# The four products of a conditioning step, side by side in the tensor engine's order

## The chip, the cores and the metric

The kernel runs on one core of a Trainium2 chip. The metric is the device time of one execution in microseconds (us); the median of three executions before the change is 3292.84 us. Five engines work beside one another: TensorE (PE in the profile; PEld is its weight load), VectorE (DVE), ScalarE (ACT), GpSimd (POOL) and SyncE (SP, which here issues all the DMA transfers; SPq is its queue). Each takes its own instructions in the order in which the program queues them.

## The reference, cut to what matters

Two transformer layers run over 1024 latent tokens and 256 context tokens, 1024 wide, in fp32. Every norm is followed by a shift, a scale and a gate that come from two conditioning vectors, one for the latent tokens and one for the context:

```python
s_x = jax.nn.silu(c)
s_c = jax.nn.silu(c_ctx)
for l in range(DEPTH):
    mod_x = (s_x @ w_mod[l] + b_mod[l])[:, None, :]
    mod_c = s_c @ w_mod[l] + b_mod[l]
    sh1_x, sc1_x, g1_x, sh2_x, sc2_x, g2_x = jnp.split(mod_x, 6, axis=-1)
    ...
    x = x + g1_x * rms_norm(m_x, norm_g[l, 1])
    f_x = squared_relu_mlp(modulate(rms_norm(x, norm_g[l, 2]), sh2_x, sc2_x), w_mlp_in[l], w_mlp_out[l])
    x = x + g2_x * rms_norm(f_x, norm_g[l, 3])
```

`w_mod[l]` is 1024 x 6144. The change is about the products `s @ w_mod` alone; the rest of the kernel computes the mixers and the MLPs.

## The kernel before

Almost all large products are dense ones: `dense()` (L377 to L384) multiplies tiles that were split into a high and a low part, three TensorE matmuls per step of 128 (L382, L383, L384), each as a rule 512 columns wide. The profile shows these as `mm`.

The conditioning products come in **rounds** (`mod_round`, L218): six of them, three per layer, each for 2048 of the 6144 columns. A round has 8 **steps**, one per 128 rows of `w_mod`. A step loads two tiles of weights, v = 0 and v = 1 (L239, SyncE's queue), 1024 columns each, and makes four products (L243 to L247): two of 512 columns from each tile. The stationary operand is `s2[:, k, :]`, 32 columns wide, of which two hold the conditioning vectors. Product g = 2v + h writes PSUM partitions 32g to 32g + 32 of one bank, `md`, and so uses columns 32g to 32g + 32 of the TensorE array. The four of a step therefore use four different column strips. A step's loop goes v = 0 first, then v = 1. The operands are plain fp32, and each product leaves two records in the trace. At the end of a round VectorE adds the biases and gains (L253 to L257), TensorE transposes the result (L260) and VectorE copies it to `mcols`, or it goes to DRAM as rows.

The rounds are spread over three stages. Round 0 of layer 0 is made in the prologue, in two halves: `parts` is ((0,), (1,)), so that a step there has two products and two tiles of 512 columns, in 32 buffers of their own. Rounds 1 and 2 of layer 0 are made in the in-projection: `rounds()` (L273) hands out one step for every third tile of tokens. The three rounds of layer 1 are made in layer 0's MLP, one step for every fifth tile, which is two steps in each of the first twelve blocks of 256 hidden columns. In these last two stages the weight tiles sit in `stg`, two staging buffers of 128 x 1024 (NSTG = 2), which the weights of the dense products (`ws`, L353) use too. A dense weight tile is read from staging by ScalarE (L186) and GpSimd or VectorE (L193), which make its high and low parts.

The order of each engine's queue is set when the program is built: a scheduler takes, at each point of its own simulated time, the ready instruction of the highest priority, and priorities follow the order in which the program was written. Nothing ties the four products of a step together, and other ready matmuls can come between them. The two places where the order is written by hand are the attention and the last block of each MLP; the rounds' products are in neither.

Of the kernel before, what the change touches and what calls it, by code (L numbers as in the profile page):

```python
# [129 lines left out]
def hybrid_dit_kernel(ctx: ExitStack, tc: tile.TileContext, x, c, cx, c_ctx, w_mod, b_mod, norm_g, w_in,  # L130
# [3 lines left out]
    pe, act, dve, pool, sp = nc.tensor, nc.scalar, nc.vector, nc.gpsimd, nc.sync  # L134
# [8 lines left out]
    def dscr(shape, name, dt=F32):  # L143
        return dram.tile(shape, dt, name=name)
# [51 lines left out]
    s2 = const.tile([128, 8, 32], F32, name="s2")  # L196
# [21 lines left out]
    def mod_round(l, r, ps, tmp, tmp_bufs, parts=((0, 1),)):  # L218

        pt = ps.tile([128, 512], F32, name="md", tag="md", bufs=1)  # L220
        bg = stg.tile([128, 2, 512], F32, tag="bg", name="bg", bufs=1)
        bt, gt = bg[:, 0, :], bg[:, 1, :]
        def biases():
            for g in range(4):
                sp.dma_start(bt[32 * g:32 * g + 32, :],
                             b_mod[l:l + 1, r * 2048 + g * 512:r * 2048 + (g + 1) * 512].to_broadcast([32, 512]))
                i = KIND[2 * r + g // 2]
                if i is not None:
                    sp.dma_start(gt[32 * g:32 * g + 32, :],
                                 norm_g[l, i:i + 1, (g % 2) * 512:(g % 2 + 1) * 512].to_broadcast([32, 512]))  # L230

        for hs in parts:
            n, h0 = 512 * len(hs), hs[0]
            for k in range(8):
                ws = []
                for v in range(2):
                    w = tmp.tile([128, n], F32, tag="stg", name="wm", bufs=tmp_bufs)
                    c0 = r * 2048 + v * 1024 + h0 * 512
                    sp.dma_start(w, w_mod[l, k * 128:(k + 1) * 128, c0:c0 + n])  # L239
                    ws.append(w)  # L240
                if hs is parts[0] and k == BIAS_AT:
                    biases()
                for v in range(2):  # L243
                    for h in hs:
                        g = 2 * v + h
                        pe.matmul(pt[32 * g:32 * g + 32, :], s2[:, k, :], ws[v][:, (h - h0) * 512:(h - h0 + 1) * 512],  # L246
                                  start=(k == 0), stop=(k == 7))  # L247
                yield
            for v in range(2):
                i = KIND[2 * r + v]  # L250
                p = slice(64 * v + 32 * h0, 64 * v + 32 * (hs[-1] + 1))
                a, g = bt[p, :], gt[p, :]
                dve.tensor_tensor(a, pt[p, :], a, op=OP.add)  # L253
                if i in (0, 2):
                    dve.scalar_tensor_tensor(a, a, 1.0, g, op0=OP.add, op1=OP.mult)
                elif i in (1, 3):
                    dve.tensor_tensor(a, a, g, op=OP.mult)  # L257
            tr = ps.tile([128, 512], F32, name="tr", tag="tr", bufs=3)
            for k in range(4):
                pe.transpose(tr[:, k * 128:(k + 1) * 128], bt[:, k * 128:(k + 1) * 128], ident)  # L260
            tr = tr.rearrange("p (k g s) -> p g s k", k=4, g=4)
            for v in range(2):
                i = 2 * r + v
                if i in (2, 5):
                    rows[l, i] = dscr([2, 2, 512], f"rows{l}{i}")
                    for s in range(2):
                        for g in range(2):
                            sp.dma_start(rows[l, i][s, g:g + 1], bt[64 * v + 32 * g + s:64 * v + 32 * g + s + 1, :])
                else:
                    for h in hs:  # L270
                        dve.tensor_copy(mcols[:, 2 * l + i // 3, i % 3, :, 4 * h:4 * h + 4], tr[:, 2 * v + h, 0:2, :])

    def rounds(l, rs, ps, every):  # L273

        steps = (x for r in rs for x in mod_round(l, r, ps, stg, NSTG))
        n = [0]

        def tick():
            n[0] += 1
            if n[0] % every == 0:  # L280
                next(steps, None)
        return tick
# [1053 lines left out]
    with tc.tile_pool(name="ps0", bufs=1, space=PSUM, reuse_waits="tile") as ps:  # L1336
        outs[0] = ex.enter_context(tc.tile_pool(name="tq", bufs=1, reuse_waits="tile"))
        with tc.tile_pool(name="tn", bufs=1, reuse_waits="tile") as tmp:
# [11 lines left out]
            with tc.tile_pool(name="m0", bufs=1, side="right", reuse_waits="tile") as m0:  # L1350
                cond_vectors(ps)
                steps = mod_round(0, 0, ps, m0, 32, ((0,), (1,)))
                for _ in range(8):
                    next(steps)
                xs = [load_x(t, ("mm", 4)) for t in al[:NF]]
                next(steps)
                for t, xt in zip(al, xs):
                    half(0, t, xt, act)
                W0 = Weights(0, True)
                loads = W0.starts(w_in[0], 1792, 512, dve)  # L1360
                for go in loads[:2]:
                    go()()
                for _ in steps:
                    pass
                for go in loads[2:]:
                    go(dve)()
# [464 lines left out]
```

## Time and profile before

| | us |
|---|---|
| median of three executions | 3292.84 |
| lowest and highest of the three | 3285.52, 3294.04 |
| the profiled execution | 3286.25 |
| its span, first to last instruction | 3284.4 |
| TensorE busy in the span | 3196.6 |
| VectorE, ScalarE, GpSimd busy | 1547.1, 1117.9, 1056.1 |

The profile's page gives busy time by engine; its views then go by stretch (each engine's busy time and TensorE's granted clock, 1.00 being 2.4 GHz), by line, and by time. In the rows by time one row is one instruction, or several of one kind that follow one another, with its start, its length and, in brackets, the idle time before it and what ended that. The lengths of matmuls overlap: what one costs in a row of them is read from start to start.

### The profile page before, as it was taken

The page shows a single profiled execution, that of the slowest core. Times are in us where ns is not written, and L with a number is a line of the kernel's source. Part 1 is how long each engine was busy: PE and PEld are TensorE (multiplying, and loading weights), DVE is VectorE, ACT ScalarE, POOL GpSimd, SP SyncE. Part 2 cuts the span into 40 slices and gives each one's busy share as a digit, 9 for nine tenths or more (in the row PEclk, how much of TensorE's full clock was granted, in tenths as well). Part 3 has the DMA queues.
Part 4 walks back from the last instruction along what each step waited for, and adds up shares of the span by engine and source line. Part 5 has one row for each costly group of instructions (what it writes and reads, how often), then busy time and mean ns, then how long its engine had stood idle before and what let it go on. Part 6 is the DMA issues. An engine that isn't in the chain of part 4 may idle for free.

```text
span 3284.4 us, 47529 instructions
## 1 busy us (share of the span) xinstructions
PE 3196.6 (97%) x18421; PEld 2611.4 (80%) x18421; DVE 1547.1 (47%) x3295; ACT 1117.9 (34%) x2315; POOL 1056.1 (32%) x878
## 2 busy tenths in 40 slices
PE   8999999999999999999999989999989999999997
PEld 3777888887887777777778878998878788888886
DVE  3345476798462343343343561148755333333335
ACT  4212576788342111111111242257864311111111
POOL 2346100035452232232232453210334533333333
PEclk9999999999999999999999999999999999999999
DMA  7566312132432222222121146124454211111113
GB/s 242 166 150 177 81 53 57 55 85 87 138 116 84 71 63 84 64 71 85 57 65 39 58 145 153 44 60 118 130 152 127 73 45 52 52 45 51 46 46 96
DMA packets 221569, 294.00 MB, mean 90 GB/s; under 512 B 36800, under 2 KB 154064, under 8 KB 221344
## 3 DMA queue, kind: packets, MB, share of 16 engines
q1 hardware_dynamic: 221248, 290.71, 30.0%
q8 instruction: 145, 2.38, 0.3%
q14 instruction: 80, 0.66, 0.1%
q0 software_dynamic: 96, 0.26, 0.0%
HBM read 240.01 MB, written 50.89 MB: 89 GB/s over the span
## 4 chain that ended last, share of the span: by engine, by line
PE 75%; DVE 3%; issue 2%; DMA 2%; POOL 1%; ACT 1%; SPq 0%; POOLq 0%; ACTq 0%; DVEq 0%
PE mm L382 20%; PE mm L383 19%; PE mm L384 19%; PE po L1081 2%; PE tp L1060 2%; PE po L913 2%; PE md L246 1%; PE S L515 1%; PE X L516 1%; PE X L515 1%; PE S L516 1%; PE po L808 1%; PE tp L892 1%; PE tp L790 1%; POOL s L193 1%
## 5 line engine op out<-in xcount | busy, mean ns | idle before, releaser
L1198 DVE TENSOR_TENSOR acc<-mm,acc 128x512 f32<-128x512 f32 x540 | 369.1, 689 | 388.1 <-PE mm L384 387.1
L193 POOL TENSOR_TENSOR r<-ws,r 128x1024 fp32r<-128x1024 f32 x146 | 356.9, 2449 | 539.5 <-ACT r L186 534.8
L384 PE MATMUL mm<-s,r 128*128 128x512 f32 (+1 forms) x1404 | 516.6, 368 | 0.0
L383 PE MATMUL mm<-s,r 128*128 128x512 f32 (+1 forms) x1404 | 515.5, 367 | 0.0
L382 PE MATMUL mm<-s,r 128*128 128x512 f32 (+1 forms) x1404 | 513.5, 366 | 1.7 <-DVE s L188 1.7
L1184 DVE TENSOR_TENSOR hr<-hr 128x512 f32<-128x512 f32 (+1 forms) x160 | 134.4, 840 | 612.7 <-ACT hr L1183 612.6
L382 PE MATMUL mm<-r,r 128*128 128x512 f32 x1046 | 413.5, 395 | 0.3 <-DVE r L188 0.3
L383 PE MATMUL mm<-r,r 128*128 128x512 f32 x1046 | 408.5, 391 | 0.0
L384 PE MATMUL mm<-r,r 128*128 128x512 f32 x1046 | 407.9, 390 | 0.0
L186 ACT ACTIVATE r<-ws 128x1024 fp32r<-128x1024 f32 x155 | 164.4, 1061 | 709.2 <-PE mm L384 336.8
L193 POOL TENSOR_TENSOR r<-hr,r 128x512 fp32r<-128x512 f32 (+1 forms) x130 | 167.0, 1285 | 562.6 <-DVE r L188 559.2
L1183 ACT ACTIVATE hr<-mm 128x512 f32<-128x512 f32 (+1 forms) x160 | 88.3, 552 | 644.4 <-PE mm L384 638.4
L382 PEld LDWEIGHTS mm<-s,r 128*128 128x128 f32 x1404 | 264.2, 188 | 50.6 <-DVE s L188 1.9
L383 PEld LDWEIGHTS mm<-s,r 128*128 128x128 f32 x1404 | 264.7, 189 | 49.2
L384 PEld LDWEIGHTS mm<-s,r 128*128 128x128 f32 x1404 | 264.1, 188 | 46.1
L382 PEld LDWEIGHTS mm<-r,r 128*128 128x128 f32 x1046 | 196.2, 188 | 80.7 <-DVE acc L1198 36.9
L384 PEld LDWEIGHTS mm<-r,r 128*128 128x128 f32 x1046 | 196.3, 188 | 43.0 <-POOL r L193 0.9
L383 PEld LDWEIGHTS mm<-r,r 128*128 128x128 f32 x1046 | 196.4, 188 | 39.1
L713 ACT ACTIVATE P<-P,nm 128x1280 f32<-128x1280 f32 (+1 forms) x160 | 190.2, 1190 | 31.1 <-DVE P L721 28.7
L382 PE MATMUL mm<-r,e 128*128 128x512 f32 (+1 forms) x496 | 192.6, 389 | 1.3 <-ACT e L186 1.3
L383 PE MATMUL mm<-r,e 128*128 128x512 f32 (+1 forms) x496 | 190.9, 385 | 0.0
L384 PE MATMUL mm<-r,e 128*128 128x512 f32 (+1 forms) x496 | 189.8, 385 | 0.4 <-POOL e L193 0.4
(256 smaller groups left out, 6011.3 us busy)
## 6 DMA issues: line engine op xcount, KB each, us to landing
wm<-in_w_mod_dram SPq DMA_DIRECT2D x80, 512.0 KB
ws<-in_w_mlp_in_dram SPq DMA_DIRECT2D x64, 512.0 KB
ws<-in_w_mlp_out_dram SPq DMA_DIRECT2D x64, 512.0 KB
q<-qT SPq DMA_DIRECT2D x224, 128.0 KB
ws<-in_w_in_dram SPq DMA_DIRECT2D x36, 512.0 KB
xres<-xn SPq DMA_DIRECT2D x18, 512.0 KB
x<-xres SPq DMA_DIRECT2D x18, 512.0 KB
wm<-in_w_mod_dram SPq DMA_DIRECT2D x32, 256.0 KB
```

The source lines that it names most:

```text
L186: act.activation(o, i, AF.Copy)
L193: lo_eng.tensor_tensor(lo, src, f(hi), op=OP.subtract)
L382: pe.matmul(pt, sh, mh, start=k == 0, stop=False)
L383: pe.matmul(pt, sh, ml, start=False, stop=False)
L384: pe.matmul(pt, sl, mh, start=False, stop=k == n - 1)
L515: pe.matmul(dst, q[0], k, start=True, stop=False)
L516: pe.matmul(dst, q[1], k, start=False, stop=True)
L713: act.activation(P, P, AF.Exp, scale=-1.0, bias=self.nm[:, u:u + 1], accum_out=self.sums[:, u:u + 1])
L913: pe.matmul(self.po, VB[self.h][:, kt, :], self.pt[:, kt, :], start=kt == self.kts[0], stop=kt == self.kts[-1])
L1183: act.activation(r, pt, AF.Relu)
L1184: dve.tensor_tensor(r, r, r, op=OP.mult)
L1198: dve.tensor_tensor(acc[t][:, s], pt, acc[t][:, s], op=OP.add)
```

## The change

In `mod_round` the four products of a step are made in the order v = 1, v = 0. The first of them keeps the place that its priority gives it. The other three are given a high priority, and each gets an edge that queues it on TensorE behind the first one (order of issue only, no wait for its end).

```diff
-                for v in range(2):
-                    for h in hs:
-                        g = 2 * v + h
-                        pe.matmul(pt[32 * g:32 * g + 32, :], s2[:, k, :], ws[v][:, (h - h0) * 512:(h - h0 + 1) * 512],
-                                  start=(k == 0), stop=(k == 7))
+
+                def group(v, h):
+                    g = 2 * v + h
+                    return pe.matmul(pt[32 * g:32 * g + 32, :], s2[:, k, :],
+                                     ws[v][:, (h - h0) * 512:(h - h0 + 1) * 512], start=(k == 0), stop=(k == 7))
+                gs = [(v, h) for v in (1, 0) for h in hs]
+                with tc.high_priority(), tc.issue_after(group(*gs[0]).ins):
+                    for x in gs[1:]:
+                        group(*x)
                 yield
```

`issue_after` adds the edges; `high_priority` raises the priority of what is traced inside it.

## Rows read from the trace of the kernel before

**Rows 1.** The page's first part: busy us, share of the span, instructions.

```profile
PE 3196.6 (97%) x18421; PEld 2611.4 (80%) x18421; DVE 1547.1 (47%) x3295; ACT 1117.9 (34%) x2315; POOL 1056.1 (32%) x878
```

**Rows 2.** Busy time by stretch (us), TensorE's clock, DMA share: prologue, in-projection, MLP.

```profile
25.00:57.00 32.00, 29.81 (x96) 11.94 (x96) 9.71 (x16) 10.15 (x25) 9.09 (x8) 0.95 0.57 206
85.00:330.00 245.00, 239.96 (x1350) 186.93 (x1350) 107.45 (x231) 54.83 (x128) 121.45 (x144) 0.99 0.59 162
985.00:1685.00 700.00, 700.00 (x3229) 536.09 (x3228) 249.55 (x371) 93.18 (x131) 189.78 (x115) 1.00 0.24 74
```

**Rows 3.** In-projection and MLP again, L246's instructions alone (PE and PEld).

```profile
85.00:330.00 245.00, 24.15 (x128) 3.35 (x128) 0.99 0.59 162
985.00:1685.00 700.00, 51.54 (x192) 7.04 (x192) 1.00 0.24 74
```

**Rows 4.** TensorE in order of time, one step in layer 0's MLP.

```profile
1053.05 0.39 PE L384 MATMUL mm<-r,r 128*128 128x512 f32 x1
1053.37 1.05 PE L246 MATMUL md<-wm,s 128*32 128x512 f32 x4
1054.35 0.50 PE L382 MATMUL mm<-r,r 128*128 128x512 f32 x1
1054.69 0.39 PE L383 MATMUL mm<-r,r 128*128 128x512 f32 x1
1054.92 0.39 PE L384 MATMUL mm<-r,r 128*128 128x512 f32 x1
...
1055.94 1.05 PE L246 MATMUL md<-wm,s 128*32 128x512 f32 x4
1056.93 0.50 PE L382 MATMUL mm<-r,r 128*128 128x512 f32 x1
```

**Rows 5.** TensorE in order of time, one step in the in-projection.

```profile
184.11 0.40 PE L384 MATMUL mm<-r,e 128*128 128x512 f32 x1
184.44 1.07 PE L246 MATMUL md<-wm,s 128*32 128x512 f32 x8
185.44 0.50 PE L382 MATMUL mm<-r,e 128*128 128x512 f32 x1
185.77 0.39 PE L383 MATMUL mm<-r,e 128*128 128x512 f32 x1
```

**Rows 6.** TensorE in order of time, end of the prologue's second half round.

```profile
52.77 1.05 PE L246 MATMUL md<-wm,s 128*32 128x512 f32 x2
53.74 0.50 PE L382 MATMUL mm<-r,e 128*128 128x512 f32 x1
...
59.14 0.66 PE L260 MATMUL tr<-ident,bg 128*128 128x128 f32 x4 [1.86 <-DVE bg L255]
```

**Rows 7.** TensorE in order of time, two groups of L246 that a transfer held up.

```profile
18.67 2.34 PE L246 MATMUL md<-wm,s 128*32 128x512 f32 x6 [1.05 <-DMA wm<-in_w_mod_dram]
...
262.25 1.92 PE L246 MATMUL md<-wm,s 128*32 128x512 f32 x4 [2.47 <-DMA wm<-in_w_mod_dram]
```

**Rows 8.** L246's weight loads: ns shortest, median, longest; first and last start.

```profile
L246 PEld LDWEIGHTS md<-wm,s x384: 106/109/178, 4.7 to 1671.1; 128*32 128x32 f32 x192
```

**Rows 9.** Layer 0's MLP: issues on SyncE's queue, in order of time.

```profile
1046.02 11.34 SPq L239 DMA_DIRECT2D wm<-in_w_mod_dram  x4
1063.72 2.90 SPq L353 DMA_DIRECT2D ws<-in_w_mlp_out_dram  x2
```

**Rows 10.** The MLP's weight tiles and their users on ScalarE, GpSimd and TensorE.

```profile
1067.24 1.06 ACT L186 ACTIVATE r<-ws 128x1024 fp32r<-128x1024 f32 x1 [22.06 <-DMA ws<-in_w_mlp_out_dram]
...
1071.15 2.39 POOL L193 TENSOR_TENSOR r<-ws,r 128x1024 fp32r<-128x1024 f32 x1 [0.32 <-ACT r L186]
...
1104.10 4.93 POOL L193 TENSOR_TENSOR r<-ws,r 128x1024 fp32r<-128x1024 f32 x2 [0.45 <-ACT r L186]
...
1104.23 0.39 PE L382 MATMUL mm<-r,r 128*128 128x512 f32 x1
...
1142.43 0.60 ACT L1183 ACTIVATE hr<-mm 128x512 f32<-128x512 f32 x1 [10.90 <-PE mm L384]
```

## The prediction

> **What bounds the kernel now.** I read the page's busy times first: TensorE works for 97% of the span, no other engine for half of it [rows 1]. The share is an average, so next came the stretches in which the rounds lie. In the MLP of layer 0, from 985 to 1685 us, TensorE is busy 700.00 of 700 us at the full clock, and VectorE, ScalarE and GpSimd for 250, 93 and 190; the transfers take 0.24 of the DMA engines' time. In the in-projection TensorE is busy 239.96 of 245 us, in the second part of the prologue 29.81 of 32 [rows 2]. Where one engine has no idle time and feeds the rest, its work is the time: what comes off its queue comes off the span. The third view is that queue itself, in order of time, around L246, and it shows what a group of these products costs. By start to start, dense matmuls follow each other every 0.23 us (1054.69 to 1054.92). With a group between them, L384 starts at 1053.05 and the second dense matmul behind the group at 1054.69: 1.64 us where two pitches would be 0.46. So **a group of two products costs 1.18 us** [rows 4]. A step in the in-projection whose four products happen to stand together spans 184.11 to 185.77, 1.66 us, so **a group of four costs 1.20 us** [rows 5]. A single product holds the queue from 52.77 to 53.74, 0.97 us, as long as two do (0.98) [rows 4, 6]. The price belongs to the group, not to the product: those on different column strips run at the same time, and 0.2 us of each group lies at its two borders with the dense matmuls.
>
> **How many groups the change removes.** Each x in these rows counts records, two per product, so x4 is half a step, x8 a whole one.
>
> MLP: 192 records [rows 3], 24 steps. Rows 4 are the pattern: two groups, the second one dense group of six matmuls later, 2.57 us from start to start. Going along the stretch I count 23 such steps, from 1002 to 1671 us (rows 4 show one of them), and one in three groups (first 991.75): 49 groups. Joined, 24. That is 25 x (1.18 + 1.18 - 1.20 = 1.16) = 29.0 us, and since TensorE never waits there [rows 2], I count all of it.
>
> In-projection: 128 records, 16 steps [rows 3]; ten are one group already as in rows 5, six are two. 6 x 1.16 = 7.0 us. TensorE has 5 us of idle time there, 2.47 of it in front of one of these pairs, whose tile had not landed, and behind that pause the pair held the queue for 1.92 us instead of 1.05, at half the clock [rows 2, 7]. In the new order the first product stands where the second pair stood, when both tiles are due: that wait may go (2.5 + 0.9 more) or one like it may come at another of the six steps. Bounds 3.5 and 10.5; I take 7.0, as most of this stretch is busy.
>
> Prologue, second half round: 8 steps of two products. Three are one group; the last five are split, ten single products, the two of a step about 1.9 us apart (rows 6 show the last but one). 5 x 1.17 = 5.9 us. The end of this round is waited for: behind it VectorE adds the biases, and the transposes L260 start at 59.14 after 1.86 us of idle time [rows 6]. If the six dense matmuls that now follow the last product are moved ahead of it, 6 x 0.23 = 1.4 us of the gain turns into a longer wait there. So between 4.5 and 5.9; below that, if the steps then wait for transfers, zero. I take 5.
>
> Prologue, first half round: TensorE waits for transfers there; the last tiles let through three products that take 2.34 us [rows 7]. Joining may save some 0.5 us, and waiting for the later tile may cost as much. I take 0.
>
> Dense matmuls, transfers, VectorE's and ScalarE's work: none is added or removed. The three edges join instructions of one queue, so they add no wait between engines.
>
> Sum: 29.0 + 7.0 + 5 = **41 us**.
>
> **What the change adds** is one wait: the first product now needs the tile v = 1, which is asked for last, and the tile v = 0 stays in its staging buffer until then, in the MLP 2.57 us longer [rows 4]. On SyncE's queue the next issues stand behind that buffer: the next step's tiles, and then the MLP's own weights at 1063.72 [rows 9]. Who waits for those? A weight tile lands 3.5 us after its issue (1063.72, read from 1067.24); its parts are made by 1073.54, and the first matmul of the next block that can use them starts at 1104.23. That is 30 us of cover. The other weights of a block are made by 1109.03, ahead of a product whose result is read at 1142.43 and which takes 24 pitches (5.5 us): 28 us of cover [rows 9, 10]. A delay of 2.6 us, twice a block, costs nothing under these. TensorE itself: the tiles are issued from 1046.02 on and the first group stands at 1053.37, 7.3 us later, against 3.5 us for a transfer [rows 4, 9, 10]. So the products stand late enough to find both tiles there.
>
> **Loads of the four strips, row and page.** Rows 5 hold four products at 1.00 us where two take 0.98. The Trainium skill (TensorE: Matmul & The Clock Gate, Part 3: Packing small matmuls) says that weight loads overlap matmuls in flight only where the row group differs, which is not so for four strips of columns, and gives 2.38x for three column tiles. By that, three products take 3 / 2.38 = 1.26 of one, an estimate worked out from that page, and four some 1.4; joined steps would cost 0.4 us more each. Rows 5 speak against it.
>
> **The rivals.**
> 1. *Four strips cost more than two.* A weight load takes 0.109 us [rows 8]. If those of the two added products didn't overlap, two records each, a joined step would take 4 x 0.109 = 0.44 us more; 30 steps of four: 13 us, a gain of 28, **3265 us**. The rule of the page above is this one. Against it: rows 5, the same four products on the same chip. Chance 0.03.
> 2. *The front gives its gain back.* In prologue and in-projection other waits end last, DMA at 0.57 and 0.59 and transposes behind VectorE [rows 2, 6, 7]. Then the MLP's 29 alone remain: **3264 us**. Chance 0.10.
> 3. *The four are not always neighbours.* The tile v = 0 or another ready instruction comes between when the order is set; half the joins fail: gain 20, **3272 us**. Chance 0.07; that nothing at all is joined, **3293 us**, 0.03. Against it: the three others need nothing but the first product and a tile asked for earlier.
> 4. *The staging buffers become the bound, and it gets slower.* Both tiles of a step are freed only by the joined four, so both loads of the next step start behind it. If the place of the next first product in TensorE's queue did not move back as far as the loads do, TensorE would stand there for a transfer, 3.5 us [rows 9, 10], in each of the 24 steps of the MLP: 84 - 41 = 43 us slower, **3336 us**. It decides when the distance from issue to product falls from 7.3 us to below 3.5. For it: the loads do move. Against it: order and loads are set together, and 3.8 us of margin. Chance 0.03.
>
> **How the numbers follow.** The profiled execution took 3286.25 us (span 3284.4, 1.85 around it), near the lowest of the three shown; the median is 3292.84. The sum gives 3286 - 41 = 3245 for that execution, 3252 against the median, which is what a later median compares with. I forecast **3252 us**, chance 0.74. Its own ends: 3245 less 8 (in-projection at its upper bound, some waits gone with the new order) is 3237; 3252 with the front's lower bounds (3.5 and 0 instead of 12) is 3261. Rivals 1, 2 and part of 3 reach to 3272, so the range is 3236 to 3272; outside lie nothing joined, the stall, and half of rival 3's cases. Faster by over 0.3% (10 us, about what a measurement of this kernel can tell from no change): 0.74 + 0.03 + 0.10 + 0.07 = 0.94. Within 0.3%: 0.03. Slower: 0.03.
>
> **What would show it.** In the changed profile L246 should stand as x8 in every step of both layers' rounds, 24 groups in the MLP and 16 in the in-projection, each about 1.0 us to the next dense matmul; the busy time of L246 in the MLP should fall from 51.5 us to about 25 [rows 3]; TensorE should still be busy throughout the MLP. A step split by dense matmuls speaks for rival 3, groups of 1.4 us for rival 1, idle time before L246 put down to the tiles for rival 4, and longer idle time before L260 or L489 for rival 2. A total outside the range with the groups joined would mean that the order set elsewhere changed as well.

## The result and the profile after

The changed kernel takes 3244.28 us (median of four executions, 3240.23 to 3246.19), the kernel before, measured again beside it, 3290.05. The ratio is 0.9865 with a 95% interval from 0.9852 to 0.9877: between 40 and 49 us less, 46 by the medians. The profiled execution of the changed kernel took 3240.23 us with a span of 3238.5, the lowest of its four.

First TensorE's queue, the view of rows 4, for a step in layer 0's MLP (the dense products are now L386 to L388):

```profile
1039.81 0.39 PE L388 MATMUL mm<-r,r 128*128 128x512 f32 x1
1040.13 1.07 PE L246 MATMUL md<-wm,s 128*32 128x512 f32 x8
1041.12 0.50 PE L386 MATMUL mm<-r,r 128*128 128x512 f32 x1
1041.46 0.39 PE L387 MATMUL mm<-r,r 128*128 128x512 f32 x1
1041.69 0.39 PE L388 MATMUL mm<-r,r 128*128 128x512 f32 x1
...
1048.16 1.06 PE L246 MATMUL md<-wm,s 128*32 128x512 f32 x8
```

The step is one group of eight records, four products, and costs 1041.46 - 1039.81 - 0.46 = 1.19 us. The next step of the block follows 8 us later, one group as well. Going along the queue there are 24 groups in the MLP, 16 in the in-projection and 8 in the prologue's second half round, where there were 49, 22 and 13.

The stretches (columns as in rows 2), then the same for L246 alone (rows 3):

```profile
25.00:57.00 32.00, 27.08 (x98) 12.87 (x96) 12.25 (x19) 11.88 (x29) 8.62 (x8) 0.82 0.57 205
85.00:330.00 245.00, 240.88 (x1435) 195.68 (x1434) 108.23 (x240) 56.19 (x133) 124.57 (x145) 0.99 0.58 162
985.00:1685.00 700.00, 700.00 (x3381) 561.45 (x3380) 259.62 (x393) 94.74 (x133) 198.43 (x121) 1.00 0.23 74
```

```profile
85.00:330.00 245.00, 17.62 (x128) 2.52 (x128) 0.99 0.58 162
985.00:1685.00 700.00, 24.50 (x184) 3.62 (x184) 1.00 0.23 74
```

TensorE is still busy throughout the MLP, and in the same 700 us it now issues 3381 matmul records instead of 3229. L246's own busy time there fell from 51.54 to 24.50 us (the first of the 24 groups lies just ahead of this window), in the in-projection from 24.15 to 17.62.

To see where the gain arises I take five instructions that both kernels have: the first score of the attention, the first ScalarE read of layer 0's MLP, the first and the last read of that MLP's last block (the one whose order is written by hand), and the last sum of layer 1's MLP. The kernel before, in order of time:

```profile
369.40 0.50 PE L515 MATMUL X<-r,q 128*128 128x512 f32 x1 [1.33 <-ACT kctx L186]
...
972.51 0.60 ACT L1183 ACTIVATE hr<-mm 128x512 f32<-128x512 f32 x1 [2.09 <-POOL s L193]
...
1852.22 0.38 ACT L1183 ACTIVATE hr<-mm 128x256 f32<-128x256 f32 x1 [0.54 <-PE mm L384]
...
1907.24 0.60 ACT L1183 ACTIVATE hr<-mm 128x512 f32<-128x512 f32 x1 [0.91 <-PE mm L384]
...
3265.71 0.68 DVE L1198 TENSOR_TENSOR acc<-mm,acc 128x512 f32<-128x512 f32 x1
```

The changed kernel:

```profile
358.48 0.51 PE L519 MATMUL X<-r,q 128*128 128x512 f32 x1 [1.33 <-ACT kctx L186]
...
961.38 0.60 ACT L1187 ACTIVATE hr<-mm 128x512 f32<-128x512 f32 x1 [2.09 <-POOL s L193]
...
1810.50 0.39 ACT L1187 ACTIVATE hr<-mm 128x256 f32<-128x256 f32 x1 [0.82 <-PE mm L388]
...
1867.24 0.60 ACT L1187 ACTIVATE hr<-mm 128x512 f32<-128x512 f32 x1 [2.45 <-POOL s L193]
...
3220.20 0.68 DVE L1202 TENSOR_TENSOR acc<-mm,acc 128x512 f32<-128x512 f32 x1
```

The changed kernel is ahead by 10.9 us at the attention, 11.1 at the MLP, 41.7 where the MLP's last block begins, 40.0 at that block's last read and 45.5 at the last sum. So prologue and in-projection gave 10.9, the attention and the output projection next to nothing, the MLP up to its last block 30.6, and what follows, in which no such product stands, another 3.8: the last block loses 1.7 of the lead, and the rest wins 5.5.

### The profile page after: what moved, and what is told of

It reads as the page before. It is cut to its first block, busy times and chain, and to the rows that moved or that the text cites. A ratio compares the mean times of both kernels' runs of the same rounds, so it can differ in the third digit from the quotient of the medians.

```text
span 3238.5 us, 47535 instructions
## 1 busy us (share of the span) xinstructions
PE 3153.1 (97%) x18421; PEld 2610.1 (81%) x18421; DVE 1538.4 (48%) x3295; ACT 1117.9 (35%) x2315; POOL 1059.0 (33%) x878
## 4 chain that ended last, share of the span: by engine, by line
PE 73%; DVE 3%; DMA 2%; POOL 2%; issue 2%; ACT 1%; SPq 0%; POOLq 0%; DVEq 0%; ACTq 0%
PE mm L386 19%; PE mm L388 19%; PE mm L387 19%; PE po L1085 2%; PE tp L1064 2%; PE po L917 2%; PE X L520 1%; PE X L519 1%; PE po L812 1%; DMA qd<-qd 1%; PE S L519 1%; PE S L520 1%; PE tp L896 1%; PE tp L794 1%; POOL s L193 1%
## 5 line engine op out<-in xcount | busy, mean ns | idle before, releaser
L388 PE MATMUL mm<-s,r 128*128 128x512 f32 (+1 forms) x1404 | 516.4, 368 | 0.0
L386 PE MATMUL mm<-s,r 128*128 128x512 f32 (+1 forms) x1404 | 514.0, 366 | 1.7 <-DVE s L188 1.7
L386 PE MATMUL mm<-r,r 128*128 128x512 f32 x1046 | 410.8, 393 | 0.6 <-DVE r L188 0.6
L388 PE MATMUL mm<-r,r 128*128 128x512 f32 x1046 | 408.0, 390 | 0.0
L386 PEld LDWEIGHTS mm<-s,r 128*128 128x128 f32 x1404 | 264.4, 188 | 50.8 <-DVE s L188 1.9
L388 PEld LDWEIGHTS mm<-s,r 128*128 128x128 f32 x1404 | 264.1, 188 | 46.2
L386 PEld LDWEIGHTS mm<-r,r 128*128 128x128 f32 x1046 | 196.7, 188 | 61.0 <-DVE acc L1202 18.4
L388 PEld LDWEIGHTS mm<-r,r 128*128 128x128 f32 x1046 | 196.7, 188 | 42.5 <-POOL r L193 0.8
L717 ACT ACTIVATE P<-P,nm 128x1280 f32<-128x1280 f32 (+1 forms) x160 | 190.3, 1191 | 30.9 <-DVE P L725 28.4
L386 PE MATMUL mm<-r,e 128*128 128x512 f32 (+1 forms) x496 | 191.7, 387 | 1.5 <-ACT e L186 0.8
L388 PE MATMUL mm<-r,e 128*128 128x512 f32 (+1 forms) x496 | 189.2, 383 | 0.4 <-POOL e L193 0.4
```

The costliest lines, as they stand in the source:

```text
L386: pe.matmul(pt, sh, mh, start=k == 0, stop=False)
L388: pe.matmul(pt, sl, mh, start=False, stop=k == n - 1)
L717: act.activation(P, P, AF.Exp, scale=-1.0, bias=self.nm[:, u:u + 1], accum_out=self.sums[:, u:u + 1])
```

## The experiments

My theory: the time follows the number of groups on TensorE's queue, each at about 1.17 us, whatever a group holds. Its rivals: each product has its own price; the gain comes from a new order elsewhere; the priority and the edges matter, not the order of the tiles. The diffs are against the changed kernel. Each ratio is to the kernel before as measured in the same session (median 3290.05, 3287.34 or 3288.50 us), so a difference of two medians of this table can be some us off. The columns behind the ratio are from each kernel's one profiled execution: how far it stands from the kernel before at four of the five instructions (us, negative is ahead; "last block" is the first read of the MLP's last block), and its groups in the prologue's second half round, in the in-projection and in the MLP.

| kernel | median us | ratio to before, 95% | attention | MLP, first | MLP, last block | last sum | groups |
|---|---|---|---|---|---|---|---|
| before | 3290.05 | 1 | 0 | 0 | 0 | 0 | 13, 22, 49 |
| changed | 3244.28 | 0.9852 to 0.9877 | -10.9 | -11.1 | -41.7 | -45.5 | 8, 16, 24 |
| joined in layer 1's rounds only | 3257.07 | 0.9891 to 0.9920 | +0.7 | +0.5 | -30.2 | -28.4 | 13, 22, 24 |
| joined in layer 0's rounds only | 3277.53 | 0.9954 to 0.9979 | -10.0 | -10.1 | -10.1 | -6.2 | 8, 16, 49 |
| not joined in the prologue | 3250.53 | 0.9876 to 0.9902 | -5.8 | -6.0 | -36.7 | -32.7 | 13, 16, 24 |
| tile v = 0 first | 3292.71 | 1.0005 to 1.0025 | +4.2 | +4.4 | +2.5 | +3.3 | 13, 32, 48 |
| order alone | 3251.26 | 0.9865 to 0.9899 | -6.8 | -6.5 | -34.6 | -36.6 | 8, 19, 26 |
| one product a step | 3246.62 | 0.9847 to 0.9885 | -10.4 | -9.3 | -40.1 | -36.7 | 8, 16, 24 |
| no products | 3215.56 | 0.9758 to 0.9793 | -10.6 | -10.4 | -66.5 | -67.2 | 8, 16, 3 |
| four single products | 3307.77 | 1.0035 to 1.0071 | -10.9 | -11.0 | +24.4 | +22.2 | 8, 16, 80 |

**Joined in layer 1's rounds only, and in layer 0's only.** For the first:

```diff
+                if l == 1:
                     gs = [(v, h) for v in (1, 0) for h in hs]
                     with tc.high_priority(), tc.issue_after(group(*gs[0]).ins):
                         for x in gs[1:]:
                             group(*x)
+                else:
+                    for v in range(2):
+                        for h in hs:
+                            group(v, h)
```

> The joined order in layer 1's rounds alone, which are made in layer 0's MLP; layer 0's rounds keep the loop of the kernel before. In the program 60 groups of these products stand on TensorE's queue, against 85 before and 49 in the changed kernel. Theory (a group costs about 1.17 us whatever it holds, and all of it lies on the path in the MLP): the MLP's 25 groups less are worth 29 to 31 us, and the 3.8 us that the changed kernel wins behind the MLP come with them if they stem from its last block's order: 3290 - 30 - 4 = 3256, or 3260 without those. Rival (the gain came from a new order elsewhere, the layer 0 stages above all): over 3270.

For the second the condition is `l == 0`.

> The joined order in layer 0's rounds alone (prologue and in-projection); layer 1's rounds keep the loop of before. 74 groups. Theory: the changed kernel stood 10.9 us ahead at the start of the attention, so 3290 - 11 = 3279; the two halves add up with the MLP-only kernel to the whole gain of 46. By the sum of the prediction it would be 3278. Rival (new order elsewhere): under 3270.

3257.07 and 3277.53, both where the groups put them. The two halves are worth 30.3 and 9.8 us against the kernel before of the same runs (3287.34), 40.1 together and not the 46 that I expected of the sum. The traces say the same more finely: the first wins 30.7 us between the MLP's first read and its last block and nothing ahead of it; the second wins 10.0 up to the attention and not 0.1 in the MLP. The further 3.8 us of the changed kernel from the last block on did not come with either half: there these two lose 1.8 and 3.9.

**Not joined in the prologue.** The same edit with the condition `len(hs) == 2`.

> As the changed kernel, but the steps of two products in the prologue keep the loop of before (the tile v = 0 first, no priority). 54 groups, five more than the changed kernel, all in the prologue. By the prediction's term it loses 5 us: 3249. Theory from the changed kernel's trace (TensorE's granted clock fell to 0.82 from 25 to 57 us, and the transposes behind the round start only 1.6 us earlier): the prologue's joins are worth 1 to 2 us, 3246. If waiting for the second tile costs more than the joins give, it is faster than the changed kernel: below 3244.

3250.53, so the expectation that I had drawn from the trace of the changed kernel, 1 to 2 us for the prologue, fell, and the prediction's term held: this kernel stands 5.8 us ahead at the attention where the changed one stands 10.9, so the prologue's joins are worth 5.1. The clock had misled me:

```profile
25.00:57.00 32.00, 29.75 (x88) 11.97 (x88) 9.35 (x15) 11.16 (x27) 9.22 (x9) 0.84 0.59 212
```

With the old order in the prologue the granted clock of that stretch is 0.84 in this execution, where it was 0.95 in the one of rows 2 and 0.82 in the changed kernel. Over the ten profiled executions it is 0.84 to 0.95 in the four kernels whose prologue steps are not joined and 0.82 to 0.93 in the six whose are. So the lower clock is no consequence of the joins, and a difference of two executions in this stretch holds only where their clocks are alike, as in the changed kernel and this one.

**Tile v = 0 first.**

```diff
-                gs = [(v, h) for v in (1, 0) for h in hs]
+                gs = [(v, h) for v in (0, 1) for h in hs]
```

> As the changed kernel, with priority and edges, but the first product is one of the tile v = 0, the tile that is asked for first. In the program the steps then stand as two pairs nearly everywhere: 94 groups, 9 more than before (the in-projection's ten joined steps of before are split too). Theory (groups): 3290 + 9 x 1.17 = 3300, and slower than before though all three tools of the change but the order are there. Rival (priority and edges alone bring the gain): about 3244.

3292.71, slower than before by 0.05 to 0.25%, and not by the 10 us that I expected. TensorE in order of time, a step of the in-projection:

```profile
143.88 0.40 PE L386 MATMUL mm<-e,e 128*128 128x512 f32 x1
144.21 1.05 PE L246 MATMUL md<-wm,s 128*32 128x512 f32 x4
145.19 0.50 PE L387 MATMUL mm<-e,e 128*128 128x512 f32 x1
...
146.78 1.05 PE L246 MATMUL md<-wm,s 128*32 128x512 f32 x4
```

Priority and edges are there, and still the step stands as two pairs: the first product goes as soon as its tile is due, the pair of the other tile is not yet ready where the order is set, and dense matmuls go between. All 16 steps of the in-projection are split so, ten more than before. That is 11.6 us by the price of a group; at the attention the kernel is only 4.2 behind. The stretch shows why:

```profile
85.00:330.00 245.00, 244.40 (x1312) 182.84 (x1309) 102.40 (x226) 52.85 (x121) 121.05 (x142) 1.00 0.59 161
```

TensorE is busy 244.40 of 245 us where it was busy 239.96 [rows 2]: 4.4 us of waits, the 2.47 of rows 7 among them, are gone, and the clock is full throughout. So ten groups at 1.16, less 4.4, is 7.2; the trace has 4.7 from the end of the prologue on. The 2.5 us between are not accounted for one by one; the pair at half clock of rows 7, 0.9 us, is part of them. The forecast of the mechanism was right, its size was not.

**Order alone.**

```diff
-                gs = [(v, h) for v in (1, 0) for h in hs]
-                with tc.high_priority(), tc.issue_after(group(*gs[0]).ins):
-                    for x in gs[1:]:
-                        group(*x)
+                for v in (1, 0):
+                    for h in hs:
+                        group(v, h)
```

> The four products in the order v = 1, v = 0 and nothing else: no raised priority, no edges. 54 groups in the program, against 49 with the whole change. Theory (groups): 3244 + 5 x 1.17 = 3250, so most of the gain comes from the order alone, since the first product waits for the tile that is asked for last and the other three are ready with it. Rival (the edges and the priority make the groups): near the kernel before, 3290.

3251.26: 37 of the 46 us come from the order of the tiles alone. What the priority adds are the last five groups: by the traces 4.1 us up to the attention, where it takes away three, and 2.5 in the MLP, where it takes away two, such as those of the first two steps in the MLP, where other matmuls come between a step's products and three stand in one group, one behind (x6 and x2):

```profile
986.80 1.06 PE L246 MATMUL md<-wm,s 128*32 128x512 f32 x6
990.77 1.05 PE L246 MATMUL md<-wm,s 128*32 128x512 f32 x2
```

The edges without the priority give the same order of every engine's instructions as the order alone, and the priority without the edges gives 49 groups in all, as the whole change does. I read these two in the order of the program's queues and did not run them.

**One product a step, and none.** In the first, steps 1 to 7 of layer 1's rounds leave out three of their four products, in the second all four; the transfers stay.

```diff
                 gs = [(v, h) for v in (1, 0) for h in hs]
+                if l == 1 and k > 0:
+                    gs = gs[:1]
```

> As the changed kernel, but in layer 1's rounds steps 1 to 7 make one product of their four; three are left out (21 steps, 63 products; the transfers stay). Groups: 49 as in the changed kernel. Theory (the price belongs to the group): a group of one takes 0.97 us to the next dense matmul where one of four takes 1.00, so 21 x 0.03 = 0.6 us less, 3243 to 3244. Rival (each product has its price, a quarter of 1.20 us): 63 x 0.3 = 19 us less, 3225.

> As the changed kernel, but in layer 1's rounds steps 1 to 7 make no product at all (84 products left out; the transfers stay). 28 groups, 21 fewer than the changed kernel. Theory: 21 x 1.20 = 25 us less, 3219. This is the price of a group measured by taking it away, with the borders in it. If other work hid part of the groups: between 3219 and 3244.

Leaving out 63 products changes the MLP up to its last block from 30.6 us gained to 30.8, 0.2 us in all; the medians, 3246.62 against 3244.28, show no gain either. TensorE in order of time:

```profile
1047.12 0.39 PE L393 MATMUL mm<-r,r 128*128 128x512 f32 x1
1047.44 1.04 PE L246 MATMUL md<-wm,s 128*32 128x512 f32 x2
1048.42 0.50 PE L391 MATMUL mm<-r,r 128*128 128x512 f32 x1
1048.76 0.39 PE L392 MATMUL mm<-r,r 128*128 128x512 f32 x1
```

From one dense matmul to the second behind the group 1.64 us, with one product as with four (1.65 above). Without the groups the MLP gains 56.1 us up to its last block (66.5 - 10.4), 25.5 more than the changed kernel: 21 groups at 1.21. The rival, a price for each product, is out: it asked for 19 us with one product left, and 0.2 came.

**Four single products.** In layer 1's rounds each product is handed out by itself, one at every tile of tokens, behind the last matmul of a dense product.

```diff
+                if l == 1:
+                    for nn, x in enumerate([(v, h) for v in (0, 1) for h in hs]):
+                        with tc.issue_after(last[0]):
+                            group(*x)
+                        if nn < 3:
+                            yield
+                    yield
+                    continue
...
-            pe.matmul(pt, sl, mh, start=False, stop=k == n - 1)
+            last[0] = pe.matmul(pt, sl, mh, start=False, stop=k == n - 1).ins
...
-            rounds(1, (0, 1, 2), ps, 5))
+            rounds(1, (0, 1, 2), ps, 1))
```

> Layer 0 as in the changed kernel; in layer 1's rounds a step's four products are handed out one at a time, each queued behind the last matmul of another dense product, so that dense matmuls stand between nearly all of them: 80 groups in the MLP (64 single products, 16 pairs) where the changed kernel has 24 and the kernel before 49. Nothing is left out. Theory (groups): 3244 + 56 x 1.17 = 3310, slower than before by 20. Rival (number of products, or order of the loads): 3244 to 3250. The two staging buffers are held for longer here; if that starves the dense products, TensorE shows idle time in the MLP and the time is above 3310.

3307.77, slower than before by 0.35 to 0.71%, with the same products and the same transfers as the changed kernel. TensorE in order of time, then the stretch:

```profile
1061.43 1.05 PE L246 MATMUL md<-wm,s 128*32 128x512 f32 x2
...
1065.36 1.04 PE L246 MATMUL md<-wm,s 128*32 128x512 f32 x2
...
1069.34 1.04 PE L246 MATMUL md<-wm,s 128*32 128x512 f32 x2
```

```profile
985.00:1685.00 700.00, 700.00 (x3076) 510.89 (x3075) 245.22 (x353) 87.30 (x122) 179.06 (x110) 1.00 0.23 69
```

From the MLP's first read to its last block it is 35.4 us slower than before, 66.0 slower than the changed kernel: 56 groups at 1.18. TensorE is busy 700 of 700 us here too, though a step holds the staging buffers over four tiles, and so no wait of TensorE comes of that.

## Why the prediction was right, point by point

- **TensorE as the bound, and no other.** Held. TensorE stays busy for 700.00 of 700 us with 49, 24 and 80 groups alike, so each group counts in full.
- **The price of a group.** Held: 1.18 to 1.20 us from rows 4 and 5; 1.19 in the changed kernel's own rows, and 1.21 and 1.18 a group from the two kernels that take groups away and add them.
- **MLP, 25 groups, 29.0 us.** 30.6 measured up to the last block and 28.9 up to that block's last read; 30.7 up to the last block in the kernel that joins only there. The pitch of a block, by its first group, went from 60.5 us (rows 4 and the same group of the next block) to 58.0.
- **In-projection, 7.0 us in bounds of 3.5 and 10.5.** With the prologue left alone the kernel is 5.8 us ahead of the kernel before at the attention, and 6.5 ahead of the one that joins in layer 1's rounds only, whose prologue ran at the same clock of 0.84 and whose in-projection has the old order. The wait of rows 7 did not go: the step that replaced that pair still waits, and here ran on at a lower clock behind it:

```profile
57.55 1.12 PE L264 MATMUL tr<-ident,bg 128*128 128x128 f32 x4 [3.78 <-DVE bg L259]
...
260.32 1.64 PE L246 MATMUL md<-wm,s 128*32 128x512 f32 x8 [2.22 <-DMA wm<-in_w_mod_dram]
```

- **Prologue, 5 us.** 5.1, as the difference of two kernels at the attention. As expected some of it became a longer wait ahead of the transposes of rows 6: 3.78 us (above) instead of 1.86, 1.9 more where the prediction allowed 1.4. Those transposes start 4.3 us earlier than in the kernel with the old prologue, whose clock was alike:

```profile
61.81 0.66 PE L269 MATMUL tr<-ident,bg 128*128 128x128 f32 x4 [1.86 <-DVE bg L264]
```

- **Four strips at the price of two (rival 1).** The rows were right: 1.00 us for four, 0.97 to 0.98 for one or two, and 0.2 us in all for 63 products more. By the Trainium skill's 2.38x for three column tiles (TensorE: Matmul & The Clock Gate, Part 3: Packing small matmuls), taken alone, four would take some 1.4 times a single product, an estimate worked out from that figure. These runs don't bear it out: for fp32 products of 512 columns they show 1.03 times.
- **The staging buffers (rival 4).** Not seen. The tiles are issued from 1031.42 on, 8.7 us ahead of their group at 1040.13. The tile that decides is v = 1, which the first product now needs; it is issued at 1033.97, 6.2 us ahead. So the distance did fall, from the 7.3 of the prediction to 6.2 to 6.5 (4.1 in the first step), but never below the 3.5 of a transfer. The block's own weights follow 1.1 us behind the second group (1048.16):

```profile
1031.42 10.60 SPq L239 DMA_DIRECT2D wm<-in_w_mod_dram  x4
1049.25 0.80 SPq L357 DMA_DIRECT2D ws<-in_w_mlp_out_dram  x2
```

- **The sum.** 41 against 41.7 where the MLP's last block begins and 40.0 at its last read. What is won from there on, 3.8 or 5.5 us, no term had, and I don't ascribe it to the change. Over the nine changed kernels the stretch from the last block to the last sum differs from before by -3.8 to +4.0 us, though its products are the same in all of them; the two that join one half each have +1.8 and +3.9. In the changed kernel's trace one part of it is a shorter wait, 3.50 us where the kernel before has 5.08 for the same transposes:

```profile
1948.55 0.69 PE L308 MATMUL tr<-ident,x 128*128 128x128 f32 x2 [5.08 <-ACT x L299]
```

```profile
1902.06 1.18 PE L312 MATMUL tr<-ident,x 128*128 128x128 f32 x6 [3.50 <-ACT x L303]
```

  Whether the order of the program or the single execution makes such a difference stays open; executions of one kernel lie several us apart as well. Against the median the forecast of 3252 was 8 us high: some 5 because the gain came out at 46 and not 41, the rest because the kernel before, measured again, had a median 2.8 us lower.

## What to carry to other kernels

Small products that can run side by side were priced here by the stretch of queue that they occupy, not by their number: read the price from start to start across the whole group, borders included, and count groups. To keep them together, let the first of them wait for the operand that arrives last; a raised priority then closes the few gaps that are left, while priority and edges behind the operand that arrives first kept none of the 40 steps of four together. Before counting a removed stretch as gain, see that the engine is busy throughout there; where it is, taking groups away and adding them moved the time by the same 1.2 us each.

## What the runs showed of the hardware

One product is as dear as four: a plain fp32 product of 32 x 512 holds the queue for 0.97 us, its two records start 0.45 us apart, and three more products on other column strips add some 0.02 to 0.03 us.

The pause in front of a late tile can cost a second time, but need not. Behind it a pair took 1.92 us instead of 1.05 [rows 7], at a granted clock of 0.50, the lower of TensorE's two levels (1.2 GHz); in the changed kernel four took 1.64 instead of 1.07, at 0.59. In the five other kernels that have such a pause at this place, of 1.87 to 2.56 us, the group behind it took 1.05 to 1.07. In two of them the clock fell just behind the group, and in three it stayed at 1.00, the longest pause among them (in-projection, prologue not joined):

```profile
266.44 1.07 PE L246 MATMUL md<-wm,s 128*32 128x512 f32 x8 [2.56 <-DMA wm<-in_w_mod_dram]
```
